# One bidirectional hybrid trunk layer on one core: the RWKV chunk step in three batches, a new column order in the last section, and solves issued ahead

## The chip, the cores and the metric

The kernel runs on one core of a Trainium2 chip. The metric is the device time of one execution in microseconds, as a median over the executions shown. Engines: PE (TensorE, with its weight loads PEld), DVE (VectorE), ACT (ScalarE), POOL (GpSimd) and SP (SyncE, which here only issues DMA).

## What is computed

One trunk layer for two groups of tokens: a prompt of 256 tokens and a sample of 2048, each with 1024 features. For both: a modulated RMSNorm, one input projection to 29 groups of 128 columns, three mixers (RWKV-7, RG-LRU, HGRN2), each scanned forward and backward over the tokens and summed, an output projection, then a second modulated norm and a gated MLP with a width-3 convolution. The prompt's scans start from zero, the sample's from given states. The final states of the prompt's scans are outputs too. The part that matters here is RWKV-7, per head and token:

```python
s_kk = einsum('bhvk,bhk->bhv', S, kk_t)
S = S * w_t - s_kk[..., None] * (kk_t * a_t) + v_t[..., None] * k_t
out_t = einsum('bhvk,bhk->bhv', S, r_t)
```

It runs over t ascending for direction 0 and descending for direction 1, for 8 heads of 64.

## The kernel before

Tokens are cut into 9 pieces q of 256 (q = 0 is the prompt), each piece into 4 chunks of 64 tokens. RWKV is computed by chunks: within a chunk the recurrence becomes products with a triangular matrix inverse, and only the 64x64 state goes from chunk to chunk.

The dense work is in fp32 split into two parts, so every dense product is three matmuls (`mm3`, L374 to L377: high by high, high by low, low by high).

Stages, in program order:

1. `dense1` (L1184): the input projection in five sections of 512 tokens (the last has 256, piece 8). Per section it goes through 29 column groups in the table `ORDER` (`ORDER0` in the first section). Groups 0 to 3 are r, 4 to 7 are k, 8 to 11 are v, for the head pairs p = 0 to 3; 12 and 13 are the low-rank inputs of decay and rate; the rest belongs to the other mixers and gates. `evac1` (L1106) takes each result out of PSUM. When v of pair p is out, `evac1` queues the pair's jobs on lane 0: `rw_prep` (L503, normalized key, with L515), `rw_shared` (L518) and `rw_job` (L543) for both directions, which end with the chunk matrices AR (L586, L588), BK and their products (L595) in DRAM. With p = 3 it queues `rw_solve` (L612) on lane 4 and `rw_fwd` (L815) on lane 1; with the last section `rw_bwd` (L1256) of piece 8 on lane 5.
2. The lanes: `run` (L1752) takes a step of `dense1` and then lets each lane step as often as its number in `RATES` says (a credit counter). What is in a lane goes one generator after another; a yield ends a step.
3. `rw_solve` inverts the triangular matrices of a section: it fetches them (written by L607), runs 31 steps of two DVE instructions (L638, L640), puts the result through DRAM, takes two sets of 32x32 products on PE (L665, L677, both in PSUM bank `e`) and writes the result for the chunk steps (L688). Its tiles have the tag `m4` with two buffers.
4. After `dense1`: lane 0 is stepped until all jobs are done, `mod_rows` (L1764, L1767 is its transpose) runs, the backward scans are queued (`add_bwd`, L1741), and `dense2` does the prompt's output projection and FFN at the rates `RATES2`, with the scans beside it. `lanes.drain` issues what is left.
5. `dense2` again for the sample, in sections of 3, 3 and 2 pieces from the end of the sequence, with the backward scans of the lower pieces beside it.

The tile framework's scheduler then decides the order on each engine. Buffers are tags with a count: a second tile of a tag with one buffer waits for the last reader of the first. PSUM has `mm` (2), `xh` (2), and `e`, `o`, `c`, `x` (1 each). r, k and v tiles of `dense1` have two buffers each. For backward chunks of pieces 6 and up a table (`ALT`) puts the tags `e` and `o` onto `xh`, and `c` onto `x`.

The chunk step `rw_chunk` (L735) goes out in five batches with a yield after each:

- the Gram products (L750, PSUM `e` and `o`), masked by DVE into the tile `gm` (L755, L757), with a copy by POOL (L754);
- eight half-height transposes of BK (L763) and two ACT copies (L767) into `bt`;
- the product pz (L775), copied by ACT to z (L777), after the old state has been copied beside v (L770, L771);
- the product pu with the inverse (L782), copied back (L784);
- the state product pS (L789), the new state S1 on DVE (L791, L792), the output products po (L796, L799, L803), and the copy of po out.

72 chunk steps run, 36 in each direction.

## Time and profile before

| | |
|---|---|
| median of 3 runs | 3968.56 us |
| all runs | 3957.85, 3968.56, 3969.95 us |
| the profiled execution | 3964.7 us, span 3962.9 us, mean clock 0.958 |
| PE busy | 3655.6 us (92%), 29752 records |
| DVE busy | 2510.5 us (63%) |
| ACT busy | 1544.1 us (39%) |
| POOL busy | 1185.7 us (30%) |

PE is busy in most of the span. The stages in time: the input projection until about 1494 us, the prompt's output projection and FFN from about 1540 to 1964 us, the sample's from 2003 us to the end. In the rows below, "PE busy" of a stretch stands beside its length, and PEclk is the granted clock as a share of the full one. Where a row says "x16", 16 records of one group run one after another.

### The profile page before, as it was taken

How to read it: one execution, taken by the hardware profiler on the slowest of the kernel's cores; microseconds unless marked ns; L12 is line 12 of the kernel's file. 1: busy time of each engine (PE TensorE's matmuls, PEld its weight loads, DVE VectorE, ACT ScalarE, POOL GpSimd, SP SyncE). 2: the span in 40 equal slices, each digit the busy share in tenths (PEclk: the TensorE clock that was granted, in tenths of full speed). 3: DMA queues.
4: the chain of work that ended last, by engine and by line, in shares of the span. 5: the costliest groups of instructions: out<-in, count | busy, mean ns of one | idle time of the engine just before them, and what ended most of it. 6: DMA issues, size and time to landing. Idle time of an engine off the chain costs nothing.

```text
span 3962.9 us, 74884 instructions
## 1 busy us (share of the span) xinstructions
PE 3655.6 (92%) x29752; PEld 3057.7 (77%) x29752; DVE 2510.5 (63%) x4919; ACT 1544.1 (39%) x2766; POOL 1185.7 (30%) x808
## 2 busy tenths in 40 slices
PE   5998999899999996899867999999989999999998
PEld 3776777667777885687656888898678999979998
DVE  4677777577677777857689455443764433376666
ACT  3455446345644755333333222222332222243333
POOL 2441221202022022234433333333433333333332
PEclk8999999989999997899989999999999999999999
DMA  7988978778877889656464232222522222242332
GB/s 252 307 271 276 272 216 250 230 203 239 250 237 234 266 269 267 179 158 187 125 214 116 80 88 80 75 82 64 175 68 64 71 65 64 64 144 80 93 94 81
DMA packets 769540, 649.12 MB, mean 164 GB/s; under 512 B 247258, under 2 KB 647974, under 8 KB 768166
## 3 DMA queue, kind: packets, MB, share of 16 engines
q1 hardware_dynamic: 736790, 610.10, 51.0%
q10 hardware_dynamic: 32400, 34.22, 2.8%
q8 instruction: 235, 3.85, 0.4%
q14 instruction: 115, 0.94, 0.1%
HBM read 481.08 MB, written 163.10 MB: 163 GB/s over the span
## 4 chain that ended last, share of the span: by engine, by line
PE 54%; DVE 12%; DMA 6%; issue 3%; ACT 3%; POOL 1%; SPq 0%; ACTq 0%; DVEq 0%; POOLq 0%
PE mm L375 8%; PE mm L377 7%; PE mm L376 7%; PE xh L375 6%; PE xh L376 5%; PE xh L377 5%; DVE m L640 1%; DVE raw L1462 1%; DVE Dn L638 1%; DVE x L1486 1%; DMA raw<-in_w_out 1%; PE e L375 1%; PE e L377 1%; PE o L375 1%; PE e L376 1%
## 5 line engine op out<-in xcount | busy, mean ns | idle before, releaser
L372 POOL TENSOR_TENSOR wlo<-raw,whi 128x1024 fp32r<-128x1024 f32 x273 | 672.1, 2464 | 972.5 <-ACT whi L371 713.4
L375 PE MATMUL mm<-hhi,whi 128*128 128x512 f32 (+2 forms) x2224 | 796.3, 359 | 25.3 <-ACT whi L371 7.7
L376 PE MATMUL mm<-hlo,whi 128*128 128x512 f32 (+2 forms) x2224 | 783.4, 352 | 6.5 <-DVE hlo L293 5.6
L377 PE MATMUL mm<-hhi,wlo 128*128 128x512 f32 (+2 forms) x2224 | 781.9, 352 | 3.9 <-POOL wlo L372 3.3
L371 ACT CAST whi<-raw 128x1024 fp32r<-128x1024 f32 x333 | 348.1, 1048 | 703.6 <-PE mm L377 297.4
L375 PEld LDWEIGHTS mm<-hhi,whi 128*128 128x128 f32 x2224 | 424.1, 191 | 84.7 <-issue 10.4
L376 PEld LDWEIGHTS mm<-hlo,whi 128*128 128x128 f32 x2224 | 424.5, 191 | 49.1 <-DVE hlo L293 6.4
L377 PEld LDWEIGHTS mm<-hhi,wlo 128*128 128x128 f32 x2224 | 424.0, 191 | 47.4 <-POOL wlo L372 4.8
L376 PE MATMUL xh<-hlo,whi 128*128 128x384 f32 (+1 forms) x824 | 272.8, 331 | 5.9 <-DVE hlo L372 3.4
L375 PE MATMUL xh<-hhi,whi 128*128 128x384 f32 (+1 forms) x824 | 274.6, 333 | 3.3 <-ACT hhi L371 3.3
L372 POOL TENSOR_TENSOR alo<-gs,ahi 128x384 fp32r<-128x384 f32 (+1 forms) x154 | 149.3, 969 | 419.0 <-ACT ahi L371 418.8
L377 PE MATMUL xh<-hhi,wlo 128*128 128x384 f32 (+1 forms) x824 | 273.0, 331 | 0.0
L1682 DVE SCALAR_TENSOR_TENSOR gs<-xh,vec,gs 128x378 f32<-128x378 f32 (+1 forms) x103 | 60.8, 591 | 328.1 <-ACT gs L1678 328.1
L1486 DVE TENSOR_TENSOR x<-xh,x 128x512 f32<-128x512 f32 x220 | 150.6, 686 | 78.8 <-PE xh L377 77.3
L1486 DVE TENSOR_TENSOR x<-mm,x 128x512 f32<-128x512 f32 x172 | 118.1, 687 | 112.2 <-PE mm L377 110.7
L1462 DVE TENSOR_TENSOR raw<-raw,g 128x1024 f32<-128x1024 f32 x98 | 134.2, 1370 | 74.0 <-DMA raw<-in_ffn_w_down 67.2
L754 POOL COPY gm<-ar 64x256 f32<-64x256 f32 x120 | 56.6, 472 | 414.9 <-PE c L799 277.4
L376 PEld LDWEIGHTS xh<-hlo,whi 128*128 128x128 f32 x824 | 156.5, 190 | 8.0 <-DVE hlo L372 3.7
L372 POOL TENSOR_TENSOR t<-t,t 128x512 fp32r<-128x512 f32 (+1 forms) x40 | 53.4, 1334 | 362.6 <-ACT t L371 200.2
L375 PEld LDWEIGHTS xh<-hhi,whi 128*128 128x128 f32 x824 | 156.4, 190 | 6.6 <-ACT hhi L371 3.6
L1688 DVE SCALAR_TENSOR_TENSOR gs<-fsg,gs 128x384 f32<-128x384 f32 (+1 forms) x154 | 119.0, 773 | 67.0 <-ACT fsg L1687 66.8
L377 PEld LDWEIGHTS xh<-hhi,wlo 128*128 128x128 f32 x824 | 156.6, 190 | 0.5
(618 smaller groups left out, 8438.8 us busy)
## 6 DMA issues: line engine op xcount, KB each, us to landing
whi<-dW SPq DMA_DIRECT2D x116, 512.0 KB, 5.1
wlo<-dW SPq DMA_DIRECT2D x116, 512.0 KB, 6.1
raw<-in_ffn_w_gate SPq DMA_DIRECT2D x88, 512.0 KB, 4.0
raw<-in_ffn_w_up SPq DMA_DIRECT2D x88, 512.0 KB, 4.0
raw<-in_ffn_w_down SPq DMA_DIRECT2D x88, 512.0 KB, 3.6
x<-in_x_sample SPq DMA_DIRECT2D x44, 512.0 KB, 6.1
raw<-in_w_out SPq DMA_DIRECT2D x40, 512.0 KB, 4.7
dAR<-AR SPq DMA_DIRECT2D x32, 512.0 KB, 5.4
```

The source lines that it names most:

```text
L371: S.copy(hi, raw)
L372: e.tensor_tensor(lo, raw, hi.bitcast(F32), op=ALU.subtract)
L375: T.matmul(out, whi, xhi, start=first, stop=False)
L376: T.matmul(out, whi, xlo, start=False, stop=False)
L377: T.matmul(out, wlo, xhi, start=False, stop=last)
L638: V.tensor_tensor(t3, L[:n, s, tr].unsqueeze(2).to_broadcast([n, nt, ncl]), X[:n, s:s + 1, cr].to_broadcast([n, nt, ncl]), op=ALU.mult)
L640: V.tensor_tensor(X[:n, tr, cr], X[:n, tr, cr], t3, op=ALU.add)
L754: G.tensor_copy(gm[H[h], :, h, 0:64], ar[H[h], :, 0, :])
L1462: V.tensor_tensor(raw, raw, g[f].unsqueeze(1).to_broadcast([128, 2, 512]), op=ALU.mult)
L1486: V.tensor_tensor(x1b[:, FS[f]], pt, x1b[:, FS[f]], op=ALU.add)
L1682: V.scalar_tensor_tensor(gv[:, :, 1:rw], pv[:, :, 0:rw - 1], cw(0), gv[:, :, 1:rw], op0=ALU.mult, op1=ALU.add)
L1688: V.scalar_tensor_tensor(gs[:, :w], sg[:, :w], 1.0, gs[:, :w], op0=ALU.add, op1=ALU.mult)
```

## The change

It has three parts.

1. `rw_chunk` is taken apart. `rw_head` loads a chunk, `rw_turn` makes four full-height transposes into PSUM `e` with one ACT copy, `rw_gram` makes the Gram products and masks. A chunk step is three batches: the transposes with pz; pu; pS with S1, the Gram of the *next* chunk, and po. The next chunk is loaded and its Gram made across piece borders too, if that piece is solved. A chunk without a Gram makes it first, in a batch of its own. The rate of lane 1 goes from 1.0 to 0.6, the ratio of batches (3 for 5).
2. The last section of `dense1` has a table of its own, `ORDER9`: 12, 13, then k, r, v of each pair, then the others.
3. After the loop that ends the jobs, lane 4 is stepped until all sections are solved, before `mod_rows` and the prompt's part are issued.

```diff
-RATES = (1.2, 1.0, 0.8, 0.6, 0.8, 1.2)
+RATES = (1.2, 0.6, 0.8, 0.6, 0.8, 1.2)
...
+    def rw_turn(bp, hd, last, tg):
+
+        tl, pt = rw_tiles(bp, tg)
+        bk = hd["ld"][1]
+        pb = pt("e", [128, 4, 128])
+        for p in range(4):
+            last = in_order(last, T.transpose(pb[:, p, :], bk[:, p, :, :].rearrange("r a x -> r (a x)"), ident))
+        hd["bt"] = tl("bt", [128, 4, 2, 64])
+        S.copy(hd["bt"].rearrange("r p h x -> r p (h x)"), pb)
+        return last
...
+    def rw_chunk(bp, d, hd, nxt, Sin, emit_o, tg={}):
+
+
+        tl, pt = rw_tiles(bp, tg)
+        H, c = RH, hd["c"]
+        ar, bk, tt, uv = hd["ld"]
+        last = None
+        if "gm" not in hd:
+            last = rw_gram(bp, d, hd, last, tg)
+            yield
+        last = rw_turn(bp, hd, last, tg)
+        gm, bt = hd["gm"], hd["bt"]
...
+        if nxt is not None:
+            last = rw_gram(bp, d, nxt, last, tg)
...
-            ld = rwF["ld"] if rwF.get("ld") else rw_loads(mp, 0, c)
-            rwF["ld"] = rw_loads(mp, 0, c + 1) if ci < 3 else None
+            hd = rwF.pop("hd", None) or rw_head(mp, 0, c)
+            nxt = None
+            if c + 1 < NCH and (ci < 3 or q and (2 * ((q + 1) // 2), 0) in solved):
+                nxt = rwF["hd"] = rw_head(mp, 0, c + 1)
...
+    ORDER9 = [12, 13] + [j + 4 * i for j in range(4) for i in (1, 0, 2)] + [19, 20, 21, 22, 23, 24, 25, 26, 15, 16, 17, 18,
+                                                                             14, 27, 28]
...
+        orders = {sec: ORDER for sec, _ in SEC1}
+        orders.update({0: ORDER0, SEC1[-1][0]: ORDER9})
+        seq = [(sec, n, j) for sec, n in SEC1 for j in orders[sec]]
...
     while len(done) < 8 * len(SEC1):
         lanes.step(0)
+    while len(solved) < 2 * len(SEC1):
+        lanes.step(4)
     mod_rows()
```

`rw_gram` is the first batch of the old step, unchanged. In all, 288 transposes and 72 ACT copies fall away; PE goes from dense products to other work less often, 70 times for chunk steps (343 to 273).

How PE's order moves is shown at three places. Numbers after a name count the program's tiles; `mm` is a dense result, L375 to L377 its three matmuls.

First, PE in the last section with the change, where 13 of the 29 column groups have been issued (`mm_15375` is the 13th, `mm_15520` the 14th). L499 is the head sum of pair 1, L665 and L677 are the solve of the section before, L554 and L595 are jobs of pair 1.

```order
L377 MATMUL mm_15375<-hhi_13821,wlo_15372 128x256
L812 MATMUL c_15398<-uv_14975,bt_15262 64x64 x8
L499 MATMUL x_15488<-t2_15484,b1r_66 128x256
L500 MATMUL x_15488<-t3_15485,b1r_66 128x256
L665 MATMUL e_15450<-Dn_15330,m4_15332 32x32 x26
...
L677 MATMUL e_15906<-m4_15748 32x32 x32
L595 MATMUL x_15795<-AR_15768,BK_15769 64x64 x5
L375 MATMUL mm_15520<-hhi_13821,whi_15516 128x256
```

The 14th group's first product thus stands behind both of pair 1's jobs. Before, r, k and v of pairs 2 and 3 came after the groups 19 to 26 and 15 to 18, and the jobs of pairs 0 and 1 stood among those.

Second, PE from the end of the input projection to the prompt's first dense product. Before (`mm_17440` is the transpose of `mod_rows`, which follows the last group `mm_17255`; L554 and L595 are jobs of pairs 2 and 3, L665 and L677 a solve):

```order
L377 MATMUL mm_17255<-hhi_14036,wlo_17252 128x256
L1767 MATMUL mm_17440<-ident_63,mod_157 96x128
...
L499 MATMUL x_16960<-t2_16956,b1r_66 128x256
...
L554 MATMUL x_17148<-lw0_14541,lrhw0_642 128x256
L555 MATMUL x_17148<-lw0_14541,lrlw_646 128x256
L665 MATMUL e_17234<-Dn_17182,m4_17184 32x32 x32
...
L677 MATMUL e_17543<-m4_17186 32x32 x32
L782 MATMUL c_17607<-mv_17605,tt_17105 64x64 x8
L375 MATMUL mm_17489<-whi_17474,hhi_17462 128x512
```

Now:

```order
L377 MATMUL mm_16927<-hhi_13821,wlo_16924 128x256
L554 MATMUL x_17057<-lw1_14011,lrhw1_643 128x256
L987 MATMUL xh_16985<-hVt_16876,hF_16886 64x64 x16
L555 MATMUL x_17057<-lw1_14011,lrlw_646 128x256
L677 MATMUL e_17104<-m4_16853 32x32 x32
L1802 MATMUL mm_17452<-ident_63,mod_157 96x128
L812 MATMUL c_17515<-uv_16451,bt_16809 64x64 x8
...
L595 MATMUL x_17084<-AR_17074,BK_17075 64x64 x8
L375 MATMUL mm_17501<-whi_17486,hhi_17474 128x512
```

Only the last job (x_17057 to x_17084) is left behind the column groups; before, the last of pair 2's and all of pair 3's were, with its head sum L499.

Third, PE in the prompt's part with the change: the last product of the last solve (L677, `e_17414`) and the first Gram of the forward chain after it (L769, in the same bank `e`).

```order
L665 MATMUL e_17379<-Dn_17373,m4_17375 32x32 x32
L375 MATMUL mm_20105<-whi_20087,ahi_19808 128x512
...
L677 MATMUL e_17414<-m4_17377 32x32 x32
L805 MATMUL x_17802<-hg1_17704,hH0_17653 64x64 x8
L375 MATMUL mm_20262<-whi_20093,ahi_19808 128x512
...
L769 MATMUL e_17527<-ar_16795,bk_16796 128x128
L769 MATMUL o_17528<-ar_16795,bk_16796 128x128
```

That Gram is for piece 6's fourth chunk and goes out with the output product of its third, whose state product (`c_17515`) stands in the piece above; before, all chunks of pieces 6 and 7 had gone by ahead of the product that answers to `e_17414`.

## Rows read from the trace of the kernel before

**Rows 1.** Windows: start:end, length, busy us (records) by engine, granted clock, DMA.

```profile
1300.00:1964.00 664.00, 584.47 (x6891) 495.11 (x6891) 467.80 (x1031) 319.61 (x630) 201.97 (x163) 0.91 0.70 210
1484.00:1606.00 122.00, 79.41 (x896) 61.43 (x896) 89.59 (x223) 63.08 (x122) 27.37 (x20) 0.72 0.90 272
1606.00:1964.00 358.00, 329.25 (x3630) 281.51 (x3629) 242.56 (x480) 141.52 (x258) 149.03 (x114) 0.95 0.55 157
2172.00:2800.00 628.00, 627.88 (x3839) 556.02 (x3838) 300.34 (x515) 169.45 (x272) 222.28 (x138) 1.00 0.29 83
2930.00:3490.00 560.00, 559.07 (x3163) 516.97 (x3164) 241.79 (x388) 146.46 (x217) 203.55 (x119) 1.00 0.23 67
```

**Rows 2.** Waits of PE, 1300 to 1964 us: releaser, us in total, times, longest.

```profile
PE x L499 <- DVE t L528: 9.2, 1, 9.2
PE c L796 <- DVE S L791: 6.8, 4, 4.3
PE e L763 <- DVE gm L757: 6.3, 3, 4.7
```

**Rows 3.** Timeline of DVE, L515 of pairs 0 to 3 and two L588.

```profile
1330.59 0.48 DVE L515 SCALAR_TENSOR_TENSOR kk<-k,vec,t 128x256 f32<-128x256 f32 x1 [1.28 <-ACT t L512]
...
1375.28 0.42 DVE L588 TENSOR_TENSOR AR<-r,ep 128x256 f32<-128x256 f32 x1
...
1389.93 0.48 DVE L515 SCALAR_TENSOR_TENSOR kk<-k,vec,t 128x256 f32<-128x256 f32 x1 [1.57 <-ACT t L512]
...
1437.33 0.48 DVE L515 SCALAR_TENSOR_TENSOR kk<-k,vec,t 128x256 f32<-128x256 f32 x1
...
1511.48 0.48 DVE L515 SCALAR_TENSOR_TENSOR kk<-k,vec,t 128x256 f32<-128x256 f32 x1
...
1537.65 0.42 DVE L588 TENSOR_TENSOR AR<-r,ep 128x256 f32<-128x256 f32 x1
```

**Rows 4.** Timeline: ACT taking out the last column group; PE, dense products of the prompt.

```profile
1493.27 0.38 ACT L1170 ACTIVATE est<-mm 128x256 f32<-128x256 f32 x1 [0.23 <-DMA dOG<-est]
...
1546.41 0.39 PE L376 MATMUL mm<-wlo,hhi 128*128 128x512 f32 x1
1546.64 0.39 PE L377 MATMUL mm<-whi,hlo 128*128 128x512 f32 x1
```

**Rows 5.** Timeline of DVE and of the queue SPq: the last solve.

```profile
1557.29 2.59 SPq L607 DMA_DIRECT2D dL<-t  x4
...
1617.53 0.19 DVE L638 TENSOR_TENSOR Dn<-m,m 128x31 f32<-128x31 f32 x1 [0.40 <-POOL m L629]
...
1665.84 0.18 DVE L640 TENSOR_TENSOR m<-m,Dn 128x31 f32<-128x31 f32 x1
...
1684.05 0.39 SPq L688 DMA_DIRECT2D dTT<-m  x1
...
1695.99 0.37 SPq L688 DMA_DIRECT2D dTT<-m  x1
```

**Rows 6.** Timeline of PE around a chunk's transposes between dense products.

```profile
1333.70 0.28 PE L375 MATMUL mm<-hhi,whi 128*128 128x256 f32 x1
1333.82 0.28 PE L376 MATMUL mm<-hlo,whi 128*128 128x256 f32 x1
1334.03 0.27 PE L763 MATMUL e<-ident,bk 64*128 64x64 f32 x1
...
1334.42 0.64 PE L404 MATMUL mm<-araw,condT 128*32 128x128 f32 x16
1335.00 0.69 PE L775 MATMUL c<-uv,gm 128*64 128x64 f32 x16
1335.61 0.39 PE L377 MATMUL mm<-hhi,wlo 128*128 128x256 f32 x1
1335.83 0.28 PE L375 MATMUL mm<-hhi,whi 128*128 128x256 f32 x1
```

**Rows 7.** Timeline of PE: four full-height transposes.

```profile
1964.58 0.60 PE L1307 MATMUL x<-ident,AR 128*128 128x128 f32 x4
```

**Rows 8.** Waits of PE, whole span.

```profile
PE e L763 <- DVE gm L757: 19.9, 9, 6.2
PE c L796 <- DVE S L791: 12.8, 11, 4.3
```

**Rows 9.** Timeline of PE: the sample's first chunk.

```profile
2002.55 0.34 PE L763 MATMUL e<-ident,bk 64*128 64x64 f32 x1 [6.22 <-DVE gm L757]
```

More of the change, by code (lines that the diff above doesn't have):

```diff
@@ L758, in rw_chunk @@
                             rkm[d][:, 64:128].unsqueeze(1).to_broadcast([128, 4, 64]), op=ALU.mult)
-        yield
-        pb = [pt("eo"[h], [128, 4, 64]) for h in range(2)]
-        for p in range(4):
-            for h in range(2):
-                last = in_order(last, T.transpose(pb[h][:, p, :], bk[H[h], p, :, :].rearrange("r a x -> r (a x)"),
-                                                  ident[H[h], H[h]]))
-        bt = tl("bt", [128, 4, 2, 64])
-        for h in range(2):
-            S.copy(bt[:, :, h, :], pb[h])
-        yield
+        return last
+    def rw_chunk(bp, d, hd, nxt, Sin, emit_o, tg={}):
+        tl, pt = rw_tiles(bp, tg)
+        H, c = RH, hd["c"]
[6 more added lines that the diff above has]
+        gm, bt = hd["gm"], hd["bt"]
         S0 = Sin[0]
```

29 lines of the change are left out of this document (17 added, 12 removed).

## The prediction

> **What bounds the kernel now.** I read the windows first, then the waits of PE, then single lines in time order. The windows [rows 1] show two kinds of stretch. In the sample's stretches PE is busy 627.88 of 628 us and 559.07 of 560 us at clock 1.00: there the time is PE's own work, and nothing that only hides a wait can help. Between 1300 and 1964 us (last section of the input projection, then the prompt's output projection and FFN beside the scans) PE is busy 584.47 of 664 us, so 79.5 us are idle. Of these 42.6 lie in the 122 us from 1484 to 1606, and 28.8 after it; 8.1 are left before. In the same 122 us the granted clock is 0.72 on average, so some of the 79.41 busy us ran at the lower level, 1.2 instead of 2.4 GHz. With 0.72 of the rate, 0.28 of 79.41 = 22 us is lost to the clock there, and 0.05 x 329.25 = 16 us after 1606. This stage, and its middle above all, is where a change of order can pay.
>
> What the waits show [rows 2]: PE waits for the products and masks of single chunk steps and jobs, 9.2 us for one v-sum, 6.3 us for a mask before a transpose (L763), 6.8 us for the state before an output product (L796). No one resource is short; PE stands because too few independent things are next in its queue. Where that comes from [rows 3]: the last head pair's preparation (L515) begins at 1511.48 and its last job ends its AR at 1537.65, whereas the last column group left PSUM at 1493.27 [rows 4]. The four L515 stand 59, 47 and 74 us apart, though pair 0's second job had its AR 45 us after its L515 (1375.28 less 1330.59). Pair 3's columns come last but three in the section, so its jobs, then the solve, then the scans run when the dense columns are used up. The last solve follows [rows 5]: its matrix goes out at 1557.29, its first DVE step is at 1617.53 (60 us later, when POOL has cleared its tile), the last step ends at 1666.02, 48.5 us on, and its two results leave at 1684.05 and 1695.99.
>
> **The change part by part.** *Work removed.* Each of 72 chunk steps had 8 half-height transposes and now has 4 full ones, and one copy less on ACT. The 8 take from 1334.03 to 1334.42, 0.39 us [rows 6]. Four 128x128 transposes of fp32 take 0.60 us for x4 with the end of the last one [rows 7]; a single row of the half-height kind lasts about 0.27, and with that for the last one the starts are (0.60 - 0.27) / 3 = 0.11 apart, 0.44 for four. Four against eight is thus 0.39 to 0.44: nothing gained or lost on PE, 72 x 0.05 = 3.6 us at most the wrong way. The Trainium skill, "TensorEngine Tiling (Array Packing)", section Overview, has it that products with a contract dimension of 64 or less gain up to 2x from tiles that run beside each other; by that at its limit, full-height ones would give up a pairing worth 28 us over the run, and the trace speaks against it, as the last rival says. ACT's 72 copies lie beside other work (ACT is busy 319.61 of 664 us here [rows 1]): nothing.
>
> *Fewer switches.* A chunk step goes out in 3 batches, not 5; the order shows PE going from dense columns to chunk work 70 times less. The price [rows 6]: from the last dense product to the transpose is 0.21 us where products stand 0.12 apart, and the first dense product after a batch takes 0.22 to the next instead of 0.12: together 0.2 us. 70 x 0.2 = 14 us. Of the 70, some 40 lie in the sample's sections, where PE is full: **-8 us** on the path. The prompt's 31 lie in a stretch with idle time, and I count them there.
>
> *Waits inside a chunk.* The transposes no longer stand right behind the Gram whose masks must empty their PSUM banks, and the next Gram stands between the state product and the output product that waits for the state. Over the whole run PE waits 19.9 us at L763 and 12.8 at L796 [rows 8]. Taking off what lies in 1300 to 1964 (6.3 and 6.8, counted below) and the first chunk of the sample, which still has no prefetched Gram (6.22, [rows 9]), leaves 7.4 + 6.0 = 13.4. Something else often is late next, so half: **-7 us** (bounds 0 and -13).
>
> *The last section's columns.* The new order projects all of r, k, v first. k, r and v have two buffers each, so pair 2's columns may be evicted only when pair 0's jobs are done, and the order shows it: after 13 of 29 groups PE has nothing but jobs and solve products until pair 1's last job (L595). Price of this new stall: 13 groups at the pace before (194 us for 29 groups, 6.7 each) would end at 1387, in truth earlier since fewer jobs lie between; pair 0's L515 moves up to perhaps 1322, pair 1's second job ends its AR 2 x 45 us later, at 1412. Between 0 (all covered by solve and job products) and 35 us idle; I take 15, as the solve's products (L665, L677), four lora products and two jobs stand there. After that, pairs 2 and 3 need no columns before them: 2 x 45 us gives 1500, against 1537.65.
>
> *Solves ahead.* The last solve is now issued before the prompt's part. Its tile is cleared and its steps stand on DVE ahead of the prompt's work; a matrix out at about 1530, 15 us until the first step (my choice; before it was 60), 48.5 us of steps and the 30 us from the last step to the second result (1666.02 to 1695.99) give 1624. PE meets the product of that solve (L665, L677) in its queue after 330 dense products of the prompt: 96 of 512 columns at 0.23 us [rows 4] and 234 of 256 at 0.12 [rows 6] make 50 us. The order has 345 other products there, mostly 64x64, each two records; 16 such records take 0.61 us (1335.00 to 1335.61 [rows 6]), so 345 x 2 x 0.038 = 26 us, and some are larger: 31. From 1515, where the last column group should end (1493 + 15 for the stall + some 6 for the jobs now in the section), that gives 1596. So PE waits 28 us there: I take 27 (bounds 5, with some of the scans' products still to do, and 45, with 33 us until the first step). The scans queued behind (forward chunks of pieces 6 and 7) are held, since all solve products go through the one bank "e" that their Gram needs; before, eight of them were done by then. They fill what was idle later, so of the 28.8 idle us after 1606 I keep 15.
>
> *Sum for 1300 to 1964.* Idle 8 + 15 + 27 + 15 = 65 against 79.5: **-15**. Clock: if the idle time is less concentrated, a third of the 22 us comes back: **-7**. Together -15 - 7 - 8 - 7 = -37 against the profiled execution, 3964.7 us: 3927.7. That execution is 3.9 below the median of the three runs (3968.56), so I put 3932 beside the median. The three runs spread by 0.3%, about 12 us, which is what can be told from no change.
>
> **The rivals.** *Absorbed.* The forward chunks held by bank "e" finish where they did, and the backward scan of piece 6, the tail and with them the prompt's end stay at 1964; idle 8 + 20 + 32 + 25 = 85 (+5), the clock as before, -8 and -7 stay: 3955 to 3959 against the profile, 3960 beside the median. For it: the last chunks of piece 8's two directions stand no earlier in the new order, counted in dense products. Against it: the dense products themselves come earlier.
>
> *Slower: the pair buffers.* The stall after group 13 is all of 35 us, the pairs stay 47 us apart [rows 3], the last job ends near 1555 and the solve's wait grows to 45: idle 8 + 35 + 45 + 27 = 115, +35.5; clock +8; -8 and -7: +28, 3993, or 3997 beside the median. For it: the buffers, which the order shows at work. Against: pair 0 needed only 45 us when the columns were there. It decides if the spacing of the four L515 does not fall below about 45 us.
>
> *Nearly all covered.* The stall is filled and the solve is early: idle 8 + 0 + 10 + 15 = 33, -46.5; clock -20; -8 and -7: -82, 3887.
>
> *The transposes double.* If two half-height transposes run at once and full-height ones cost one after the other as much as two, 0.39 more x 72 = 28 us, and my sum becomes -9: 3960. The rows speak against it, since four full ones took what eight halves took. The rule on tiles of the Trainium skill named above, at its limit, would give this case.
>
> That the change does not do what it says is ruled out by the order: the solves' products do stand ahead and the columns do come first.
>
> **How the numbers follow.** Forecast 0.55 (own range 3910 to 3952), absorbed 0.15, pair buffers 0.20, nearly all covered 0.06, transposes 0.04. Faster by over 0.3% (below 3956.7): forecast, full cover, and a little of the absorbed case, 0.62. Slower (above 3980.5): the pair buffers and their near neighbours, 0.21. The rest, 0.17, is the same. The range 3895 to 3988 leaves out the full cover and the dearer half of the pair-buffer case.
>
> **What would show it.** Right: four L515 less than 45 us apart; the last column group out of PSUM near 1515 and the last AR by about 1510; last solve out before 1640; idle in the stretch that answers to 1300-1964 near 65; PE idle before L677 of the last solve near 27; four transposes in 0.39 to 0.44. Wrong: idle after group 13 above 30; the wait at the last solve above 45; the sample stretches longer than 628 and 560 us, which no part of the sum foresees; or the prompt's last product again at 1964.

## The result and the profile after

| | before | changed |
|---|---|---|
| median, us (4 runs each) | 3963.20 | 3996.38 |
| lowest and highest, us | 3957.81 and 3969.95 | 3993.81 and 3999.76 |
| profiled execution, us (span) | 3964.7 (3962.9) | 3999.76 (3998.0) |
| mean clock in it | 0.958 | 0.952 |

The changed kernel takes 1.0092 times as long [1.0071, 1.0113]. It is slower by 0.9%, where 3932 us and "faster" were forecast.

Where the time went is read best in four parts of the span, cut at the same dense products: up to the first dense product of the last section, the last section, the prompt's part up to the first dense product of the sample, and the sample. The kernel before, windows as in [rows 1] (start:end, length, busy us and records of PE, PEld, DVE, ACT, POOL, granted clock, DMA share, GB/s):

```profile
0.00:1282.70 1282.70, 1162.76 (x10961) 875.97 (x10961) 892.96 (x1868) 614.09 (x1121) 290.77 (x220) 0.96 0.82 249
1282.70:1540.60 257.90, 221.96 (x2931) 187.39 (x2926) 195.94 (x469) 168.53 (x360) 37.76 (x42) 0.89 0.85 266
1540.60:2002.80 462.20, 385.21 (x4161) 324.70 (x4159) 307.32 (x639) 170.75 (x311) 173.56 (x131) 0.90 0.61 178
2002.80:3962.90 1960.10, 1885.64 (x11708) 1669.65 (x11707) 1114.25 (x1945) 590.78 (x975) 683.66 (x416) 0.98 0.30 91
```

The changed kernel, the same four parts, then the whole stage that answers to 1300 to 1964 of before, its two pieces, and the stretch between the 13th and the 14th column group:

```profile
0.00:1294.60 1294.60, 1169.12 (x10779) 880.46 (x10779) 889.19 (x1861) 613.79 (x1094) 295.06 (x218) 0.95 0.81 246
1294.60:1544.10 249.50, 214.72 (x2817) 183.21 (x2813) 177.98 (x421) 134.13 (x295) 36.47 (x40) 0.90 0.81 248
1544.10:2056.50 512.40, 406.88 (x4264) 343.10 (x4264) 332.60 (x693) 206.03 (x356) 183.36 (x135) 0.86 0.60 176
2056.50:3998.00 1941.50, 1868.93 (x11612) 1665.67 (x11608) 1112.55 (x1944) 587.88 (x954) 677.25 (x416) 0.98 0.30 92
1300.00:2013.00 713.00, 605.85 (x6963) 515.16 (x6963) 483.40 (x1056) 328.29 (x628) 213.33 (x170) 0.89 0.67 200
1300.00:1606.00 306.00, 249.01 (x3044) 209.66 (x3044) 212.19 (x495) 154.85 (x325) 59.68 (x54) 0.86 0.81 249
1606.00:2013.00 407.00, 356.84 (x3920) 305.51 (x3920) 271.21 (x562) 173.44 (x303) 153.66 (x117) 0.91 0.56 164
1409.20:1438.50 29.30, 17.73 (x342) 14.37 (x342) 14.08 (x34) 9.93 (x26) 1.51 (x3) 0.57 0.81 238
```

So the 35 us are +12 before the last section, -8 in it, +50 in the prompt's part and -19 in the sample. In 1300 to 2013, which ends at the prompt's last dense product as 1964 did before, PE is idle 713.00 - 605.85 = 107 us against 79.5. Up to 1606 that is 57 (before: 50.7); after 1606 it is 50 (before: 28.8).

The four L515 and the last column group, DVE and ACT in time order, answer to [rows 3, 4]:

```profile
1340.07 0.48 DVE L515 SCALAR_TENSOR_TENSOR kk<-k,vec,t 128x256 f32<-128x256 f32 x1 [2.40 <-ACT t L512]
...
1408.88 0.48 DVE L515 SCALAR_TENSOR_TENSOR kk<-k,vec,t 128x256 f32<-128x256 f32 x1 [4.61 <-ACT t L512]
...
1456.38 0.48 DVE L515 SCALAR_TENSOR_TENSOR kk<-k,vec,t 128x256 f32<-128x256 f32 x1 [1.41 <-ACT t L512]
...
1505.34 0.48 DVE L515 SCALAR_TENSOR_TENSOR kk<-k,vec,t 128x256 f32<-128x256 f32 x1 [1.04 <-ACT t L512]
...
1531.12 0.38 ACT L1200 ACTIVATE est<-mm 128x256 f32<-128x256 f32 x1 [0.99 <-ACT m L671]
```

They stand 69, 47 and 49 us apart (59, 47, 74 before), and the columns end 38 us later than before. The last solve, on the queue SPq, POOL and DVE, answers to [rows 5]; L626 on the queue reads the second half of its matrix back, and L628 on POOL clears its tile:

```profile
1552.10 2.57 SPq L607 DMA_DIRECT2D dL<-t  x4
...
1581.00 1.34 SPq L626 DMA_DIRECT2D m<-dL  x1
...
1589.82 0.95 POOL L628 MEMSET m<- 128x1024 f32 x1 [2.33 <-ACT m L627]
...
1594.25 0.18 DVE L638 TENSOR_TENSOR Dn<-m,m 128x31 f32<-128x31 f32 x1
...
1665.29 0.37 SPq L688 DMA_DIRECT2D dTT<-m  x1
```

Its matrix goes out 5 us earlier than before, its first step is 23 us earlier, and its second result leaves at 1665.29 instead of 1695.99. What PE waits for in 1300 to 2013 (line, releaser: us in total, times, longest), which answers to [rows 2]:

```profile
PE c L812 <- DVE uv L807: 13.2, 6, 4.1
PE mm L1598 <- ACT kk L1589: 12.4, 2, 8.7
PE mm L375 <- ACT whi L371: 11.3, 3, 6.5
...
PE c L821 <- DVE S L814: 4.6, 1, 4.6
```

At the solve's products (L665, L677) PE waits 0.6 us in this stretch, so they are not among them. PE stands before the prompt's norm (L1598) and its first dense products, and at steps inside single chunks (L812, the state product, waits for the `uv` that the batch before it writes).

**When the dense work is done.** Start of the n-th matmul of the dense products (L375 to L377, three to a product), counted in program order and the same in all kernels, against before:

| dense matmul | what it is | before, us | changed | columns alone (e3) | columns without the stall (e13) |
|---|---|---|---|---|---|
| 2784 | last section begins | 1282.7 | +12 | -1 | +7 |
| 3096 | its 14th column group | 1381.8 | +57 | +43 | +10 |
| 3479 | its last | 1482.7 | +48 | +34 | +10 |
| 3480 | prompt's output projection | 1540.6 | +4 | +6 | -16 |
| 3576 | prompt's FFN | 1618.7 | -13 | +11 | +1 |
| 4100 | | 1792.3 | -2 | +15 | +12 |
| 4200 | | 1819.5 | +43 | +14 | +10 |
| 4895 | prompt's last | 1964.3 | +48 | +20 | +12 |
| 4896 | sample's first | 2002.8 | +54 | +31 | +24 |

Two jumps show. At the 14th group dense products stand still while the pairs' buffers come free; but the time is back when the prompt begins, because the 58 us between the section's last matmul and the prompt's first (1482.7 to 1540.6) have shrunk to 13. Then, from matmul 4100 to 4200, 72 us go by (27 before).

### The profile page after: what moved, and what is told of

Read it like the earlier page. It is cut to its first block, busy times and chain, and to the rows that moved or that the text cites. A ratio compares the mean times of both kernels' runs of the same rounds, so it can differ in the third digit from the quotient of the medians.

```text
span 3998.0 us, 74266 instructions
## 1 busy us (share of the span) xinstructions
PE 3659.7 (92%) x29464; PEld 3072.4 (77%) x29464; DVE 2512.3 (63%) x4919; ACT 1541.8 (39%) x2696; POOL 1192.1 (30%) x808
## 4 chain that ended last, share of the span: by engine, by line
PE 57%; DVE 16%; DMA 9%; ACT 4%; issue 3%; SPq 1%; POOL 1%; ACTq 0%; DVEq 0%; POOLq 0%
PE mm L375 8%; PE mm L376 8%; PE mm L377 8%; PE xh L375 5%; PE xh L377 5%; PE xh L376 5%; DVE Dn L638 1%; DVE x L1521 1%; DVE m L640 1%; DVE raw L1497 1%; PE c L798 1%; PE e L375 1%; PE e L769 1%; PE e L376 1%; PE e L377 1%
## 5 line engine op out<-in xcount | busy, mean ns | idle before, releaser
L375 PE MATMUL mm<-hhi,whi 128*128 128x512 f32 (+2 forms) x2224 | 800.2, 360 | 29.3 <-ACT whi L371 8.8
L377 PE MATMUL mm<-hhi,wlo 128*128 128x512 f32 (+2 forms) x2224 | 784.7, 353 | 4.9 <-POOL wlo L372 4.2
L375 PEld LDWEIGHTS mm<-hhi,whi 128*128 128x128 f32 x2224 | 428.2, 193 | 85.6 <-issue 11.9
L377 PEld LDWEIGHTS mm<-hhi,wlo 128*128 128x128 f32 x2224 | 428.2, 193 | 48.4 <-POOL wlo L372 5.6
L375 PE MATMUL xh<-hhi,whi 128*128 128x384 f32 (+1 forms) x824 | 272.5, 331 | 5.2 <-ACT hhi L371 5.2
L377 PE MATMUL xh<-hhi,wlo 128*128 128x384 f32 (+1 forms) x824 | 272.0, 330 | 0.0
L375 PEld LDWEIGHTS xh<-hhi,whi 128*128 128x128 f32 x824 | 155.8, 189 | 7.6 <-ACT hhi L371 5.6
L377 PEld LDWEIGHTS xh<-hhi,wlo 128*128 128x128 f32 x824 | 155.8, 189 | 0.7
```

The lines of the kernel that those rows point to most:

```text
L375: T.matmul(out, whi, xhi, start=first, stop=False)
L377: T.matmul(out, wlo, xhi, start=False, stop=last)
```

## The experiments

Ratios are to the kernel before on the same chip, with 95% intervals. Lengths "last section" and "prompt's part" are those of the windows above (257.9 and 462.2 before, 249.5 and 512.4 changed).

### Each part alone

**e4: the chunk step alone** (part 1; the lines are against the changed kernel).

```diff
-        orders.update({0: ORDER0, SEC1[-1][0]: ORDER9})
+        orders.update({0: ORDER0})
...
-    while len(solved) < 2 * len(SEC1):
-        lanes.step(4)
```

> The kernel before with the first part alone (chunk step in three batches, lane rate 0.6). Theory A: within 10 us of before, 3953 to 3973, with the first columns in e and o next to the forward chunks of piece 8 (83 products without a dense one there). Theory B: a gain of about 15 us from fewer switches and waits, 3945 to 3955. Theory C: slower by about 30 us, 3985 to 4000.

Measured: 1.0017 [1.0001, 1.0032]. Its window of the sample:

```profile
2023.30:3964.50 1941.20, 1868.43 (x11610) 1667.07 (x11608) 1112.02 (x1944) 587.71 (x954) 677.29 (x416) 0.98 0.30 92
```

The sample takes 1941.2 us, as in the changed kernel: the 19 us there are part 1's. But the first part grows from 1282.7 to 1294.4, the last section to 261.6 and the prompt's part to 467.3, and the gain is gone.

**e3: the columns alone** (part 2 in the kernel before).

```diff
+    ORDER9 = [12, 13] + [j + 4 * i for j in range(4) for i in (1, 0, 2)] + [19, 20, 21, 22, 23, 24, 25, 26, 15, 16, 17, 18,
+                                                                             14, 27, 28]
```

> The kernel before with the second part alone (r, k, v columns first in the last section). Theory A: PE stalls after the 13th group by some 40 us, but gets it back before the prompt's first column, because the jobs no longer stand behind the section; 3955 to 3970. Theory B: slower by about 30 us, 3985 to 4000. Theory C: a gain, 3945 to 3960.

Measured: 1.0066 [1.0044, 1.0088]; last section 265.5, prompt's part 487.1.

**e2: the solves alone** (part 3 in the kernel before).

```diff
+    while len(solved) < 2 * len(SEC1):
+        lanes.step(4)
```

> The kernel before with the third part of the change alone (all solves issued before the prompt's part). Theory A: the forward chunks of pieces 6 and 7 wait for bank e until the last solve, and in PE's order 152 products without a dense one stand at the place where the prompt's columns first use e; slower than before by 10 to 40 us (3975 to 4003). Theory B and C: this part is a gain, 3940 to 3960.

Measured: 1.0141 [1.0117, 1.0164], dearer than the whole change and than any of the ranges. The window of its prompt's part:

```profile
1532.40:2049.90 517.50, 411.89 (x4285) 347.50 (x4279) 324.34 (x669) 186.95 (x341) 171.41 (x131) 0.85 0.56 165
```

The prompt's part is 55 us longer than before, with 105.6 us idle (77.0 before) and a granted clock of 0.85 (0.90 before).

**e7: parts 1 and 2, without the solves ahead** (against the changed kernel).

```diff
-    while len(solved) < 2 * len(SEC1):
-        lanes.step(4)
```

> The change without its third part (chunk step and columns, solves where they were). Theory D: the forward chunks aren't held; the stall after the 13th group is there but is made good before the prompt; 3960 to 3980. Theory B: 3985 to 4005, as the columns' part remains.

Measured: 1.0072 [1.0044, 1.0100]. Alone the parts cost 0.17, 0.66 and 1.41%; all three together cost 0.92%, not 2.2, and the third adds 0.2 to the first two, inside the intervals. The traces show what may be one reason: with the new columns and the new step the last solve, left where it was, comes later than before (its second result leaves at 1745.65 in e7, at 1695.99 before), and issuing it ahead takes that back (1665.29). That what is left is small because the chains are late in the same place is a reading, not shown.

### Which single wait is it?

In the changed kernel four things of RWKV end late in the prompt's part. The state update S (L815) ends a chunk. On DVE, in time order: the third and the fourth forward chunk of piece 6, before and after the solve, the last backward chunk of piece 7, the last forward chunk of piece 8, the first and the last backward chunk of piece 6:

```profile
1535.77 0.42 DVE L815 TENSOR_TENSOR S<-S,WC 128x256 f32<-128x256 f32 x1
...
1682.94 0.42 DVE L815 TENSOR_TENSOR S<-S,WC 128x256 f32<-128x256 f32 x1
...
1793.49 2.57 DVE L815 TENSOR_TENSOR S<-S,WC 128x256 f32<-128x256 f32 x1
...
1847.89 0.43 DVE L815 TENSOR_TENSOR S<-S,WC 128x256 f32<-128x256 f32 x1
...
1908.39 0.43 DVE L815 TENSOR_TENSOR S<-S,WC 128x256 f32<-128x256 f32 x1
...
1980.43 1.08 DVE L815 TENSOR_TENSOR S<-S,WC 128x256 f32<-128x256 f32 x1
```

No forward chunk is done for 147 us, piece 8's last comes at 1848 (1773 before), piece 6's first backward one at 1908 (1861 before): in the code `rw_bwd` of piece 6 takes over the buffer `on0` from piece 8, so it waits for piece 8's tail, and that for its forward chunks. Also, the prompt's FFN uses the banks `e` and `o` from its column JX = 8 on, and stands behind those forward chunks there.

**e1: the FFN uses `e` and `o` later.**

```diff
-        GRP, PRE, LVS, JX = 2, 2, 2, 8
+        GRP, PRE, LVS, JX = 2, 2, 2, 10
```

> The changed kernel with one number changed: the prompt's FFN begins to put dense columns into the PSUM banks e and o at column 10 instead of 8. Theory A (banks): in the changed kernel the dense columns in e and o stand in PE's order behind the last forward chunk steps, which hold e and o and which the solves ahead have made late; PE loses about 50 us between 1790 and 1863 us. Then this kernel takes about 3950 us (3940 to 3962), and the dense columns 10 to 12 of the prompt run between the last forward chunk steps. Theory B (pair buffers): what is lost is the stall after the 13th column group of the last section (about 45 us behind the kernel before at that point), given on to the end; this kernel stays at 3996 (3988 to 4002). Theory C (chunk batches): the chunk step with the prefetched Gram is itself slower; this kernel stays above 3980.

Measured: 1.0092 [1.0063, 1.0120], no change. Matmul 4200 was now 2 us earlier than before (changed: 43 later), so the jump is gone, and yet the sample's first dense matmul came at 2044.3, 41.5 later than before: the loss returned within 700 matmuls.

**e5: e1, and a buffer of its own for piece 6** (`on6`, put onto the tag `m4` in the table `BG`).

```diff
...
-        yield from until(lambda: q in (0, NPC - 2) or (q + 2 if q < NPC - 1 else 0) in tailed)
-        on = rwB["on", q] = nt(f"on{q % 2}", (128, 4, 4, 64), 1)
+        yield from until(lambda: q in (0, NPC - 2, SEC2[0][0]) or (q + 2 if q < NPC - 1 else 0) in tailed)
+        on = rwB["on", q] = nt("on6" if q == SEC2[0][0] else f"on{q % 2}", (128, 4, 4, 64), 1)
```

> The changed kernel with the banks e and o used from column 10 on (as in the first experiment, which alone gained nothing) and a buffer of its own for the outputs of piece 6's backward chunks (tag m4, free after the last solve), so that they needn't wait for the tail of piece 8. Theory D (scan chain): the prompt's stage ends by a chain: forward chunks of pieces 6, 7, 8, then the tail of piece 8, which frees the buffer, then the backward chunks of piece 6, then its tail. The solves ahead hold the forward chunks at bank e for some 147 us, so the chain is late. With this edit piece 6's backward chunks follow piece 7's at about 1800 instead of 1912, and the time is 3950 to 3975. Theory B (pair buffers): the 48 us lost after the 13th column group are given on; 3985 to 4000. Theory A (banks) has fallen as the sole cause, since the first experiment removed the stall and not the loss.

Measured: 1.0083 [1.0064, 1.0101]. Piece 6's first and last backward chunk on DVE:

```profile
1809.97 0.42 DVE L815 TENSOR_TENSOR S<-S,WC 128x256 f32<-128x256 f32 x1
...
1862.30 0.41 DVE L815 TENSOR_TENSOR S<-S,WC 128x256 f32<-128x256 f32 x1
```

They are 118 us earlier at the end, and the prompt's part is 503.8 still. The chain over that buffer is real, and not the price by itself. Two things meet at the sample's first dense matmul. One is the last output of piece 6's tail, here of before and of the changed kernel:

```profile
1986.51 1.39 ACTq L1321 DMA_DIRECT2D dMX<-t  x2
```

```profile
2040.31 1.27 ACTq L1356 DMA_DIRECT2D dMX<-t  x2
```

The sample's first matmul follows 16 us later in both (2002.81 and 2056.55), and the chain that ended last runs over this output. In e5 it leaves at 1963.91, 76 us earlier than in the changed kernel, but the sample begins at 2042.27, only 14 us earlier: the other thing, the prompt's own last dense matmul, comes at 2008.0 (2012.6 changed), the chain that ended last runs over that one here, and in no run does the sample begin less than 34 us after it.

**e6: the forward scan steps between the solves.**

```diff
     while len(solved) < 2 * len(SEC1):
         lanes.step(4)
+        lanes.step(1)
```

> The changed kernel, where the loop that issues the solves ahead also steps lane 1 (the forward chunks), so that they take turns at bank e. Theory D: the forward chunks of piece 6 follow each other without the 147 us break, the last of piece 8 is done by about 1800 instead of 1848, piece 6's backward chunks begin some 40 us earlier; 3955 to 3975. Theory B: the pair buffers' stall is unchanged, 3985 to 4000.

Measured: 1.0083 [1.0066, 1.0099]. Piece 8's last forward chunk is back at 1778 and the prompt's part at 500.6. So three single waits are taken away, each with its effect seen where it was, and none moves the time by more than 0.1%, which is inside the intervals.

All three are waits of RWKV. In the changed kernel the last RG-LRU job and the backward scans of HGRN and RG-LRU are queued only behind the solves, on lane 2. RG-LRU's last forward output (`dLA`) and HGRN's last backward output (`dMX` from `hF`) in the changed kernel, then the latter in e6:

```profile
1800.75 0.38 SPq L1103 DMA_DIRECT2D dLA<-hQ  x1
...
1968.20 0.65 ACTq L1404 DMA_DIRECT2D dMX<-hF  x1
```

```profile
2024.37 1.49 ACTq L1404 DMA_DIRECT2D dMX<-hF  x2
```

Before, they leave at 1520.87 and 1673.74. e6 frees the forward scan and makes these still later: the chain that ended last runs there over HGRN's output. What lane 2 costs in the changed kernel was not tried; e15 below tries it with the solves alone.

### The columns: the stall, or what is moved behind it?

**e13: the columns without the stall.** In the last section, two pairs share one 512-wide k, r or v buffer, so all four pairs have one.

```diff
+    def pair_tile(tag, p, n):
+        if n == 2:
+            return mt(tag, (128, 512), 2)
+        if p % 2 == 0:
+            half[tag] = mt(tag, (128, 512), 2)
+        return half[tag][:, PC * (p % 2):PC * (p % 2) + PC]
```

> The columns' part alone, with the stall taken away: in the last section, whose tiles are half as wide, two pairs share one buffer of k, r and v, so all four pairs have room. In PE's order the run of 147 products after the 13th group is gone, and HGRN's jobs stand where they stand with the columns alone. Theory B (stall): the 0.66% goes, 3955 to 3970. Theory E (HGRN and RG-LRU late): most of it stays, 3980 to 3995.

Measured: 1.0060 [1.0046, 1.0074], as e3 within the interval. Its windows of the last section and the prompt's part:

```profile
1289.80:1524.70 234.90, 208.58 (x2650) 178.31 (x2646) 168.78 (x404) 132.61 (x292) 38.39 (x42) 0.90 0.83 263
1524.70:2026.80 502.10, 407.40 (x4440) 340.05 (x4440) 339.88 (x704) 207.30 (x379) 170.93 (x131) 0.87 0.61 179
```

The stall is gone (14th group +10 instead of +43) and the section is 23 us shorter than before. The prompt's part takes that and more: 40 us longer, with 22 us more busy time of PE and 18 more idle.

What comes later in the new order is HGRN and RG-LRU, whose columns now stand behind all pairs. HGRN's last forward output (`dHO`) leaves at 1456.84 before, 1548.28 changed, 1540.95 in e3 and 1520.33 in e13. Two orders that separate stall and lateness:

**e9: HGRN and RG-LRU first, then the pairs** (stall kept).

```diff
+    ORDER9 = [12, 13, 19, 20, 21, 22, 23, 24, 25, 26, 15, 16, 17, 18, 4, 0, 8, 5, 1, 9, 6, 2, 10, 7, 3, 11, 14, 27, 28]
```

> The kernel before with another column order in the last section: 12, 13, then 19 to 26 (HGRN) and 15 to 18 (RG-LRU), then k, r, v of the four pairs in a row, then 14, 27, 28. It keeps the stall at the pair buffers and makes HGRN's and RG-LRU's columns early. Theory E (other lanes): what the columns' part costs is that HGRN's last job begins late (its output at 1541 instead of 1457 us), so that the HGRN and RG-LRU scans run in the prompt's part beside the RWKV scans; here they are early, 3955 to 3970. Theory B (stall at the pair buffers): 3980 to 3995, as with the columns alone.

Measured: 1.0098 [1.0076, 1.0121]; last section 305.5, prompt's part 443.6. HGRN was early (1445.76) and the prompt's part the shortest of all kernels run, but the pairs had become late in turn and the section paid 48 us. It shows that what is put last pays, and does not tell stall and lateness apart.

**e10: pairs as before, HGRN last.**

```diff
+    ORDER9 = [4, 0, 12, 13, 8, 5, 1, 9, 15, 16, 17, 18, 14, 27, 28, 19, 6, 2, 10, 20, 21, 22, 23, 7, 3, 11, 24, 25, 26]
```

> The kernel before with the pairs where they were in the last section (eight groups between pairs 1 and 2, four between 2 and 3), but the HGRN groups 19 to 26 swapped behind 15 to 18, 14, 27, 28, so that the last of them ends the section. No stall, HGRN late. Theory E: 3975 to 3995. Theory B: 3955 to 3968.

Measured: 1.0092 [1.0074, 1.0111]; last section 244.2, prompt's part 500.7. Without a stall, and with HGRN's output at 1603.15, one moved mixer costs as much as the whole change.

**e17: pairs early, HGRN where it was, RG-LRU behind** (RG-LRU's groups come three places later than before, not six; pair 3's four earlier).

```diff
+    ORDER9 = [12, 13, 4, 0, 8, 5, 1, 9, 19, 20, 21, 22, 23, 24, 25, 26, 6, 2, 10, 7, 3, 11, 15, 16, 17, 18, 14, 27, 28]
```

> The kernel before with a milder column order in the last section: 12, 13, pairs 0 and 1, the HGRN groups 19 to 26, pairs 2 and 3, then 15 to 18, 14, 27, 28. Pair 3 comes four groups earlier than before, HGRN where it was, only the RG-LRU groups later by six; no run without dense products after the 13th group. Theory E (late HGRN jobs are the price of the columns' part): within 8 us of before, 3955 to 3971. If the RG-LRU groups or any disturbance of the order cost the same: 3980 to 3995.

Measured: 1.0044 [1.0026, 1.0061]; last section 260.0, prompt's part 473.5. The queue's rows for HGRN's last output, of before, e17, e13 and e10 in this order:

```profile
1456.84 0.42 SPq L991 DMA_DIRECT2D dHO<-hF  x1
```

```profile
1455.65 0.38 SPq L991 DMA_DIRECT2D dHO<-hF  x1
```

```profile
1520.33 0.50 SPq L991 DMA_DIRECT2D dHO<-hF  x1
```

```profile
1603.15 0.33 SPq L991 DMA_DIRECT2D dHO<-hF  x1
```

With the columns alone, the cost goes up with this time: 1455.65 costs 0.44%, 1520.33 costs 0.60, e3's 1540.95 costs 0.66, 1603.15 costs 0.92 (neighbouring intervals overlap, those of the two ends do not; e9, with 1445.76 and 0.98%, stands outside, as its pairs are late). That fits the lateness of HGRN as part of the price. The 0.44% of e17 is not explained by HGRN's forward output, which is on time there. But RG-LRU's last output leaves 20 us later than before (1540.89 against 1520.87), and HGRN's backward scan, on the same lane, ends 51 us later (1725 against 1674). That RG-LRU is the cause was not tried alone.

### The solves: what is queued behind them?

Issued ahead, all solve products stand in the queues before the steps of the other lanes. Letting lanes step in turn with lane 4 tells which of them paid.

**e14: in turn with the forward scan** (lane 1).

```diff
+    while len(solved) < 2 * len(SEC1):
+        lanes.step(4)
+        lanes.step(1)
```

> The solves' part alone, in turns with lane 1 only (forward chunks). Alone the part costs 1.4%, with turns of lanes 1 and 2 0.4%. If the forward chunks held at bank e are the price: 3965 to 3985. If HGRN and RG-LRU behind the solves are the price: 3995 to 4020.

Measured: 1.0070 [1.0056, 1.0084].

**e15: in turn with RG-LRU and its like** (lane 2, its last job and the backward scans queued before the loop).

```diff
+    lanes.add(2, lru_job(NPC - 1))
+    add_bwd(SEC2[0], 5, 2, 2, 0)
+    while len(solved) < 2 * len(SEC1):
+        lanes.step(4)
+        lanes.step(2)
```

> The solves' part alone, in turns with lane 2 only (last RG-LRU job, HGRN and RG-LRU scans); the forward chunks stay behind the solves at bank e. If the forward chunks are the price: 3995 to 4020. If HGRN and RG-LRU are: 3965 to 3985. If both hold the end of the prompt's part by themselves, neither this nor the turns of lane 1 alone gains more than half: both 3990 to 4015.

Measured: 1.0088 [1.0071, 1.0105].

**e11: in turn with both** (all three in the kernel before, as e2; the first two lines are moved up from behind `mod_rows`).

```diff
+    lanes.add(2, lru_job(NPC - 1))
+    add_bwd(SEC2[0], 5, 2, 2, 0)
+    while len(solved) < 2 * len(SEC1):
+        lanes.step(4)
+        lanes.step(1)
+        lanes.step(2)
```

> The kernel before with the third part alone, changed: the last RG-LRU job and the backward scans are queued before the loop, and the loop steps lanes 4, 1 and 2 in turn, so that forward chunks, HGRN and RG-LRU go out between the solves' steps. Theory E: solves alone cost 56 us because everything else of the scans stands behind them in the in-order queues and at bank e; with turns that is gone, 3940 to 3965. Theory F (the early solves themselves disturb, whatever stands behind): 3990 to 4015.

Measured: 1.0036 [1.0023, 1.0049]. The window of its prompt's part:

```profile
1531.80:2008.80 477.00, 381.65 (x4210) 324.77 (x4208) 303.42 (x649) 172.44 (x317) 169.88 (x131) 0.88 0.60 175
```

Against e2 (1.41%), turns with lane 1 give back 0.71 points, with lane 2 0.53, with both 1.05. Three quarters of the price of solving ahead is thus what stood behind the solves, not the solves. With lane 2 in turn the backward scans of HGRN and RG-LRU also go out earlier: HGRN's three backward pieces end between 1732 and 1824 in e2 and between 1564 and 1625 in e11 (1575 to 1674 before). The 0.36% that is left stays open; the prompt's part is 15 us longer still.

### Looking for the better kernel

**e8: the chunk step with the buffer for piece 6** (e4 with the buffer of e5, JX = 8).

```diff
...
-        on = rwB["on", q] = nt(f"on{q % 2}", (128, 4, 4, 64), 1)
+        on = rwB["on", q] = nt("on6" if q == SEC2[0][0] else f"on{q % 2}", (128, 4, 4, 64), 1)
```

> The chunk step alone (as in the fourth experiment, 3967) with the own buffer for piece 6. Theory D: the chain by the tail of piece 8 binds the kernel before too, at a smaller price (43 us between the last backward chunk of piece 7 and the first of piece 6); with it cut the prompt ends some 15 us earlier; 3940 to 3958. Theory B: no change, 3962 to 3972.

Measured: 3950.89 us against 3960.49, 0.9980 [0.9967, 0.9992]. It beats both kernels, by a little. Its windows without the last section (the profiled execution took 3960.28 us, the longest of the ten):

```profile
0.00:1297.80 1297.80, 1170.37 (x10779) 880.68 (x10779) 888.50 (x1861) 614.24 (x1094) 296.01 (x218) 0.95 0.81 245
1557.90:2018.00 460.10, 385.95 (x4260) 324.80 (x4258) 318.46 (x658) 172.26 (x294) 177.95 (x133) 0.90 0.62 184
2018.00:3958.50 1940.50, 1869.48 (x11610) 1667.28 (x11608) 1104.85 (x1944) 589.02 (x954) 676.71 (x416) 0.98 0.30 92
```

The sample keeps its 20 us; 15 of them go in the first part, and the prompt's part is as long as before (e4: 467.3).

**e18: that buffer alone** (in the kernel before).

```diff
...
-        on = rwB["on", q] = nt(f"on{q % 2}", (128, 4, 4, 64), 1)
+        on = rwB["on", q] = nt("on6" if q == SEC2[0][0] else f"on{q % 2}", (128, 4, 4, 64), 1)
```

> The kernel before with the own buffer for piece 6's backward outputs alone. If the gain of the eighth experiment (0.2% faster than before, where the chunk step alone is 0.2% slower) is the buffer's: 3945 to 3957. If it needs the chunk step in three batches: 3958 to 3968.

Measured: 1.0004 [0.9992, 1.0015]: nothing. It takes both, chunk step and buffer. In the traces the buffer brings piece 6's last backward chunk from 1950 to 1920 us with the new step (e4, e8), and only from 1928 to 1925 with the old one (before, e18); why the old step gains so little is not settled.

**e16: e8 with the turns of e11.**

```diff
+    lanes.add(2, lru_job(NPC - 1))
+    add_bwd(SEC2[0], 5, 2, 2, 0)
+    while len(solved) < 2 * len(SEC1):
+        lanes.step(4)
+        lanes.step(1)
+        lanes.step(2)
```

> The chunk step with the own buffer for piece 6 (0.2% faster than before) and the solves ahead in turns with lanes 1 and 2; the column order of before. If the turns take the whole price of the solves' part away: 3940 to 3955. If what they leave (0.4% alone) adds up: 3960 to 3975.

Measured: 1.0036 [1.0024, 1.0049]. The solves ahead cost the better kernel 0.56 points, even in turns.

**e12: e16 with another column order**: four HGRN groups ahead of pairs 0 and 1, four behind them, the RG-LRU groups between pairs 2 and 3.

```diff
+    ORDER9 = [12, 13, 19, 20, 21, 22, 4, 0, 8, 5, 1, 9, 23, 24, 25, 26, 6, 2, 10, 15, 16, 17, 18, 7, 3, 11, 14, 27, 28]
```

> The three parts in a mended form: the chunk step in three batches; in the last section 12, 13, four HGRN groups, pairs 0 and 1, four more HGRN groups, pair 2, the RG-LRU groups, pair 3, the rest; solves ahead in turns with lanes 1 and 2; the own buffer for piece 6's backward outputs. Theory E: each of the held lanes is free, 3920 to 3945. Theories B and F: 3960 or more.

Measured: 1.0047 [1.0032, 1.0063]; last section 274.4, prompt's part 456.6. A miss: against e16 (1.0036) the order gains nothing, and no kernel with another order beat the one before.

## Why the prediction was wrong

The profiled executions differ by +35 us where -37 was summed, an error of 72. By the terms of the sum:

| term | predicted | measured |
|---|---|---|
| before 1300 | 0 | +12 |
| idle, 1300 to 1606 | 8 + 15 + 27 = 50, from 50.7 | 57 |
| idle after 1606 | 15, from 28.8 | 50 |
| busy time of the stage, clock included | -7 | 605.85 - 584.47, less 12 of work from the part before: +9 |
| after the prompt's last product | -8 and -7 | -13 (+48 there, +35 at the end) |

**The step that failed** is "They fill what was idle later, so of the 28.8 idle us after 1606 I keep 15". The scans that were held back did not fill the idle time: 50 us are idle there, 35 more than the 15 kept, and the chain that ended last runs over the end of the scans. The text knew of the forward chunks behind bank `e` and priced their delay as a gain. Windows from the first dense matmul of the prompt's FFN to the prompt's last one, of before, the changed kernel, e2, e11 and e7 in this order:

```profile
1618.70:1964.30 345.60, 320.40 (x3565) 275.04 (x3564) 231.98 (x453) 137.28 (x251) 145.45 (x110) 0.97 0.55 158
```

```profile
1605.80:2012.60 406.80, 356.69 (x3920) 305.71 (x3920) 271.01 (x562) 173.44 (x303) 153.84 (x117) 0.91 0.56 164
```

```profile
1591.70:2002.50 410.80, 360.03 (x3901) 308.68 (x3902) 265.02 (x529) 151.08 (x281) 146.73 (x115) 0.89 0.55 159
```

```profile
1634.10:1958.50 324.40, 302.69 (x3284) 262.70 (x3282) 190.81 (x357) 130.09 (x234) 141.77 (x105) 0.95 0.56 162
```

```profile
1628.60:2000.40 371.80, 330.15 (x3608) 285.62 (x3605) 259.19 (x537) 138.48 (x237) 148.13 (x112) 0.93 0.57 166
```

e2 and e11 show the step by itself. With the solves ahead alone PE is idle 51 us here (25 before); with the held lanes stepping in turn 22, and the cost falls from 1.41 to 0.36%. In the changed kernel it is 50, but in e7, without the solves ahead, still 42. So the solves ahead are enough to make the idle time, but without them the new columns with the new step make most of it too, and which scan does it there stays open. The columns alone do not make it (26 in e3 and in e13). What they cost, 0.60% without a stall (e13), is spread over the prompt's part, and e10 shows a part of the cause: HGRN's columns, moved to the end without a stall, cost 0.92%. That its work then lies in a part with fewer dense columns to cover it is a reading, not shown by itself.

**The stall after group 13** was placed right, and nearly priced right: 11.6 us idle (29.30 - 17.73 in the window above) against the 15 taken. The rest of those 29 us is job and solve work at a granted clock of 0.57. The idle time is not the price: the time is back at the prompt's first product, and e13, without it, gains 0.06 points, inside the interval.

**The wait at the solve** of 27 us at L665 and L677 did not come. The solve's result was later than worked out (1665.29 against 1624, as its matrix went out 22 us later than the 1530 taken and the first step came 42 us after that and not 15). The wait before the first step was put down to the clearing of its tile, but most of it is the matrix's way back: its second half is read only 29 us after it went out (47 before: 1604.42), and the clearing follows that. But the prompt's dense work was late as well, held by waits on `kk` and `whi` (12.4 and 11.3), and its FFN began at 1606. The idle time up to 1606 comes to 57 us where 50 were summed, but by other waits: that the size came near is luck, and the mechanism did not hold.

**The pair buffers.** This rival named 3997 us and had its condition met, with 69, 47 and 49 us between the L515. The number is near 3996.38, by other terms: it asked for 35 us of idle time at the stall (11.6), 45 at the solve (no wait there), and 27 after 1606 (50). e13 takes its mechanism away and leaves the columns' price. Its chance, 0.20, was given to a story that the runs do not bear out.

**Fewer switches and waits inside a chunk** were right in sign and too small in the sample: 170 passages from dense products to chunk work became 139 (31 fewer, where some 40 were taken), and PE's busy time there fell by 17 us, its length by 19, against -8 and a share of -7. By 0.2 us a passage the 31 would give 6; what the other 11 us of busy time are, no run tells. e4 shows that all of it is the chunk step's. Of the two waits the second did go, the first did not. Waits of PE over the whole span, which answer to [rows 8]:

```profile
PE e L757 <- DVE gm L776: 26.1, 11, 6.1
...
PE c L821 <- DVE S L814: 5.5, 3, 4.6
```

The wait for the masks, now before the full-height transposes (L757), is 26.1 us against 19.9; the wait for the state before the output products is 5.5 against 12.8. Together 31.6 against 32.7. Without the stage and the sample's first chunk, as the prediction counted, 13.4 became 19.0, where 7 was to come off.

**The transposes** were priced at 0 to 0.05 us more a step. The timeline of PE in the changed kernel, the four and what follows:

```profile
1791.22 0.60 PE L757 MATMUL e<-ident,bk 128*128 128x128 f32 x4
1791.75 0.72 PE L798 MATMUL c<-uv,gm 128*64 128x64 f32 x15
```

From the first transpose to the next product is 0.53 us, the median over the steps of the changed kernel and of e4 in which the four stand together (68 and 67 of 72); for the eight half-height ones it is 0.40, over the 23 steps of before in which nothing stands between them. By these medians that is 0.13 x 72 = 9 us, not 3.6. The sum gave the fourth the 0.11 us that lie between the starts of the others, but the next product starts 0.20 after it (0.53 - 3 x 0.11). The rival that they double (0.39 more a step) had the direction right and a third of the size: here the full-height ones cost 1.3 times the eight halves. The Trainium skill, "TensorEngine Tiling (Array Packing)", section Overview, has up to 2x for products with a contract dimension of 64 or less; the trace agrees with the direction, with 1.3x.

**The 12 us before the last section** were in no term. The chunk step makes them: the first part takes 1293.5 us in the mean of the nine kernels with it, and 1284.2 in the eleven without. That is 9 us, one execution each; the 12 are those of the profiled pair. 22 chunk steps run there in the changed kernel, so the transposes make 22 x 0.13 = 3 of them; what the rest is stays open.

What held: the stall's place and its idle time, the sign of the gain in the sample, and that the clock of the prompt's part fell as its idle time rose (0.86 granted with 105.5 us idle, 0.90 before with 77.0), though the other way than forecast. The idle time alone does not set it: e5 has 0.88 with 104.3.

## What to carry to other kernels

If the dense columns are the cover of the scans, as I read them here: before moving one mixer's columns forward, list what is moved back, and price that by when its last output leaves, not by the idle time that it might fill. Issuing a long chain ahead delays everything queued behind it; let the held lanes step in turn with it (1.41% became 0.36%), or leave it where it was. And when several chains end late in the same stretch, taking away one wait shows its effect at its place and nothing in the total (e1, e5, e6), so a total that does not move is no proof that the wait was not there: look which output the next stage waits for, and what stands just behind it.

## What was not expected of the hardware

- Full-height fp32 transposes of 128x128: four take 0.53 us to the next product, eight of 64 rows in two banks 0.40 us (medians).
- In the 29.3 us from 1409.2 to 1438.5, in which PE had job and solve products and no dense one, it was busy 17.73 us and the granted clock was 0.57 on average, so some 86% of the stretch ran at the lower level of 1.2 GHz ((1 - 0.57) / 0.5). Before, in 1300 to 1400, with jobs between dense columns, it was 0.94.
- The solve's first DVE step came 42 us after its matrix had left on the queue (60 before). Of these, 29 went by until the read of its second half was issued on the same queue (1581.00), and 13 until it had landed, was copied by ACT and the tile was cleared by POOL.
